# Who makes the low parts of two raw weight blocks, in a fast block product of a decoder layer

## The chip, the cores and the metric

The kernel runs on one core of a Trainium2 chip. The metric is the time of one execution in microseconds (us). TensorE (PE in the profile, PEld its weight loads) multiplies, VectorE (DVE) and ScalarE (ACT) work on SBUF and PSUM, GpSimd (POOL) on SBUF, and SyncE (SP) issues nearly all transfers.

## The reference, cut to what matters

One decoder layer over 1024 rows of width 1024. The part that matters here is a set of dense products, and what is done to their results:

```python
u = rmsnorm(x, norm_mix) @ w_in          # retention gate rg, LRU lx and ly, branch gates: columns of w_in
hl = rg_lru_branch(lx, ...); o_l = hl * gelu(ly)
merged = (g[:, :, 0] * (od @ w_branch[0]) + g[:, :, 1] * (o_r @ w_branch[1])
          + g[:, :, 2] * (o_l @ w_branch[2]))
x = x + merged @ w_out
```

Everything is float32. Attention, retention, cross-attention and the squared-ReLU MLP stand before and after these products and are not touched.

## The kernel before, in words

**Three passes.** A float32 product is made of reduced-precision matmuls: each operand is split into a high part, which is a cast on ScalarE (line 70), and a low part, the operand minus its high part, which is one subtraction (line 71) on an engine that the caller names. Each 128-row step is then three matmuls in a row (lines 59 to 61): high by high, high by low of the right operand, low by high of the left one. So the third matmul of a product is the first that needs the low part of the weights.

**Seven products for eight.** From about 660 us to 1510 us of the span the products are made in pairs of weight units. A pair is a 2x2 arrangement of raw blocks A11, A12, A21, A22 of 128x512 elements; instead of eight block products there are seven (numbered k = 1 to 7), with sums of blocks as left operands. Product 1 uses A11 itself, product 2 uses A12, product 4 uses A22, and products 5, 6, 7, 3 use the sums S1, S2, S3, S4. Each product is four steps of three matmuls into one PSUM tile; six such tiles go round.

**The sums.** `left` (line 1064) makes the four sums on VectorE: S1 = A21 + A22 into a tile of its own; S3 = A11 - A21 over A21; S2 = S1 - A11 over A11; S4 = A12 - S2 over A12. Two of the raw blocks, A11 and A12, are thus overwritten by S2 and S4. S2 can only be written when the high and the low part of A11 have been made, S4 when those of A12 have been.

**Low parts.** `pair` (line 1082) passes the engine `lo` on to `product` (line 1104) and that to `pair_unit` (line 1094), which splits the left operand. In the input projections `lo` is GpSimd for all seven; in the branches (`branch`, line 792) it is VectorE for products 6 and 4 and GpSimd for the other five.

**The results.** `product` combines the seven PSUM tiles on VectorE as they come (lines 1125, 1127 and 1130 add PSUM to an SBUF tile of sums, ScalarE copies the first at line 1121) and hands the four blocks of the output to `emit`. A PSUM tile is free again when VectorE has read it.

**Order of the pairs.** There are 23 pairs in the projections: four for the retention gate, eight for the LRU (every second one from the third on) and eleven for the branch gates; then 12 pairs in the three branches, four each. In the steady part the seven products run in the order 1, 2, 6, 7, 5, 4, 3; where two pairs share each right-hand block (the first and the last two pairs of the projections, and two pairs of each branch) in the order 1, 2, 3, 7, 6, 5, 4. Between LRU pairs stands the recurrence: ScalarE makes sigmoids (line 633), GpSimd a product (line 634), ScalarE tanh, exp and sqrt with table loads (lines 635 to 637), VectorE lines 638 and 639, the scan (line 640) and line 641.

**Order on the queues.** The kernel is written in a framework whose planner sets the order of the instructions on each engine from its own estimates when the kernel is built; from then on each engine takes its queue in that order, and waits where an input is not ready. The casts of the weight units are tied to each other in the order of the source. Raw blocks come through three staging tiles; SyncE's queue holds the load of the next unit until a staging tile has been read for the last time.

Of the kernel before, what the change touches and what calls it, by code (L numbers as in the profile page):

```python
# [49 lines left out]
class Kernel:  # L50
# [1031 lines left out]
    def pair(self, p, k, c, units, right, psum, emit, lo):  # L1082

        if k == 1:
            st = self.sf[:, 6:8, :].rearrange("p k c -> p (k c)") if p % 2 else None
            c["w"] = self.raw_pair(units, st)
            c["t"] = self.sf[:, 2 * p % 4, :], self.sf[:, 2 * p % 4 + 1, :]
        if "left" not in c and 1 in c and 2 in c:
            c["left"] = True
            w = c["w"]  # L1090
            self.left(w, self.sf[:, 4 + p % 2, :], w["A11"], w["A12"], self.nc.vector)
        self.product(k, c, right, psum, lo, emit)

    def pair_unit(self, src, lo):
        if self.n_units % 2 == 0:
# [302 lines left out]
```

## Time and profile before

| | us |
|---|---|
| median of three runs | 2461.78 (2456.99 to 2462.23) |
| the profiled execution | 2457.39 |
| its span, first to last instruction | 2455.6 |
| TensorE busy in it | 2320.9 (95%) |
| VectorE busy | 1854.2 (76%) |
| GpSimd busy | 1091.8 (44%) |
| ScalarE busy | 1044.8 (43%) |

Busy time is what an engine spends in instructions; a wait for another engine is not counted. The granted clock (PEclk) is the share of TensorE's full clock that it was given. Names as `wu<-st` are the tile written and the tiles read: `wu` is a split weight unit, `st` a staging tile, `sf` the tile that holds sums, every second pair's second unit and the partial results.

### The profile page before, as it was taken

The numbers are of one execution on the slowest core, as the hardware profiler recorded it, in microseconds if no ns is written. First come the engines' busy times: TensorE is split into PE (matmuls) and PEld (weight loads), VectorE is DVE, ScalarE is ACT, GpSimd is POOL, SyncE is SP. The second block draws the span as 40 slices with busy tenths as digits, with TensorE's granted clock in tenths as the row PEclk, the third lists the DMA queues.
The fourth block names the chain that finished last, engine by engine and source line by source line (L and its number), as shares of the span: only waits on it lengthen the run. The fifth ranks groups of instructions, "written<-read, shape, count | busy, mean of one in ns | idle before, by whom it ended". The sixth has DMA issues, their size and how long they took to land. (4 is left out here: it accounts for less than half of the span.)

```text
span 2455.6 us, 31231 instructions
## 1 busy us (share of the span) xinstructions
PE 2320.9 (95%) x11132; PEld 1908.8 (78%) x11132; DVE 1854.2 (76%) x2850; ACT 1044.8 (43%) x1823; POOL 1091.8 (44%) x714
## 2 busy tenths in 40 slices
PE   9999999999998999999998987999989999999996
PEld 7888878888876877777876766788768888778884
DVE  7677387877786776786677898345788888788888
ACT  5444355555545454445244443135432222343333
POOL 1122212221216555566542334034155555698787
PEclk9999999999999999999999988999999999999999
DMA  4222222222225345453676776343325444734431
GB/s 170 80 86 70 65 61 69 66 64 62 61 56 195 119 162 171 140 178 112 208 252 211 256 263 193 112 162 104 106 80 175 150 156 141 274 138 172 158 138 74
DMA packets 137259, 338.28 MB, mean 138 GB/s; under 512 B 17152, under 2 KB 27393, under 8 KB 137104
## 3 DMA queue, kind: packets, MB, share of 16 engines
q1 hardware_dynamic: 136528, 334.44, 41.4%
q8 instruction: 89, 1.46, 0.2%
q10 hardware_dynamic: 576, 1.84, 0.2%
q14 instruction: 66, 0.54, 0.1%
HBM read 229.21 MB, written 98.63 MB: 134 GB/s over the span
## 5 line engine op out<-in xcount | busy, mean ns | idle before, releaser
L59 PE MATMUL ps<-block,wu 128*128 128x512 f32 x1428 | 570.7, 400 | 53.8 <-DVE sf L1125 21.5
L61 PE MATMUL ps<-block,wu 128*128 128x512 f32 x1428 | 567.8, 398 | 11.4 <-POOL wu L71 6.2
L60 PE MATMUL ps<-block,wu 128*128 128x512 f32 x1428 | 564.4, 395 | 1.7 <-POOL block L71 1.0
L71 POOL TENSOR_TENSOR wu<-st,wu 128x512 fp32r<-128x512 f32 x214 | 323.3, 1525 | 317.5 <-ACT wu L70 317.4
L59 PEld LDWEIGHTS ps<-block,wu 128*128 128x128 f32 x1428 | 272.9, 191 | 118.1 <-issue 19.5
L61 PEld LDWEIGHTS ps<-block,wu 128*128 128x128 f32 x1428 | 272.8, 191 | 79.2 <-POOL wu L71 11.0
L60 PEld LDWEIGHTS ps<-block,wu 128*128 128x128 f32 x1428 | 272.9, 191 | 62.8 <-DVE block L71 1.6
L70 ACT CAST wu<-st 128x512 fp32r<-128x512 f32 x240 | 141.2, 618 | 166.6 <-DVE st L1066 71.3
L71 POOL TENSOR_TENSOR w<-st,w 128x1024 fp32r<-128x1024 f32 x50 | 123.7, 2485 | 158.3 <-ACT w L70 158.2
L59 PE MATMUL ps<-wu,hu 128*128 128x512 f32 x448 | 177.2, 395 | 17.1 <-DVE acc L1198 14.3
L61 PE MATMUL ps<-wu,hu 128*128 128x512 f32 x448 | 174.8, 392 | 3.6 <-DVE hu L71 3.6
L60 PE MATMUL ps<-wu,hu 128*128 128x512 f32 x448 | 175.5, 392 | 0.0
L1198 DVE TENSOR_TENSOR acc<-acc,ps 128x512 f32<-128x512 f32 x216 | 137.8, 678 | 20.4 <-PE ps L61 19.9
L71 POOL TENSOR_TENSOR wu<-sf,wu 128x512 fp32r<-128x512 f32 x63 | 116.7, 1866 | 67.9 <-ACT wu L70 57.3
L71 DVE TENSOR_TENSOR hu<-sth,hu 128x1024 fp32r<-128x1024 f32 x56 | 121.1, 2167 | 20.9 <-ACT hu L70 20.2
L466 ACT ACTIVATE p<-sc,mx 128x256 f32<-128x256 f32 (+7 forms) x128 | 94.8, 741 | 71.1 <-DVE mx L463 49.2
L59 PEld LDWEIGHTS ps<-wu,hu 128*128 128x128 f32 x448 | 84.7, 189 | 41.3 <-DVE acc L1198 12.4
L61 PEld LDWEIGHTS ps<-wu,hu 128*128 128x128 f32 x448 | 84.7, 189 | 22.6 <-DVE hu L71 4.9
L59 PE MATMUL psk<-block,w 128*128 128x512 f32 x256 | 101.7, 397 | 0.0
L61 PE MATMUL psk<-block,w 128*128 128x512 f32 x256 | 101.2, 395 | 0.0
L60 PE MATMUL psk<-block,w 128*128 128x512 f32 x256 | 100.8, 394 | 0.0
L60 PEld LDWEIGHTS ps<-wu,hu 128*128 128x128 f32 x448 | 84.7, 189 | 17.2 <-POOL wu L71 0.4
(389 smaller groups left out, 5608.0 us busy)
## 6 DMA issues: line engine op xcount, KB each, us to landing
sth<-h SPq DMA_DIRECT2D x56, 512.0 KB, 9.4
st<-in_w SPq DMA_DIRECT2D x32, 512.0 KB, 4.3
h<-hab SPq DMA_DIRECT2D x32, 512.0 KB, 2.8
w<-in_w SPq DMA_DIRECT2D x8, 2048.0 KB
sgb<-gsp SPq DMA_DIRECT2D x48, 256.0 KB, 4.4
gsp<-l SPq DMA_DIRECT2D x44, 256.0 KB, 2.1
acc<-y SPq DMA_DIRECT2D x40, 256.0 KB, 3.8
st<-in_w_br SPq DMA_DIRECT2D x18, 512.0 KB, 5.5
```

The source lines that it names most:

```text
L59: nc.tensor.matmul(ps, lhsT=lhs.hi, rhs=rhs.hi, start=start, stop=False)
L60: nc.tensor.matmul(ps, lhsT=lhs.hi, rhs=rhs.lo, start=False, stop=False)
L61: nc.tensor.matmul(ps, lhsT=lhs.lo, rhs=rhs.hi, start=False, stop=stop)
L70: ins = self.nc.scalar.copy(dst.hi, src)
L71: self.lo_ins = (lo_engine or self.nc.vector).tensor_tensor(dst.lo, src, f32(dst.hi), op=ALU.subtract)
L466: nc.scalar.activation(p[:, 0:n], sc[:, 0:n], AF.Exp, bias=mx, accum_out=l)
L1198: eng.tensor_tensor(acc[k][:, st, :], acc[k][:, st, :], x if isinstance(x, bass.AP) else acc[x][:, st, :], op=ALU.add)
```

## The change: what it does

In `pair`, the engine that makes the low part becomes VectorE where k is 1 or 2, whatever the caller passed; for the other five products it stays what it was. 35 pairs with two products each are concerned, so 70 subtractions of 128x512 elements. The MLP does not go through `pair` and keeps its engines.

```diff
         if "left" not in c and 1 in c and 2 in c:
             c["left"] = True
             w = c["w"]
             self.left(w, self.sf[:, 4 + p % 2, :], w["A11"], w["A12"], self.nc.vector)
-        self.product(k, c, right, psum, lo, emit)
+
+        self.product(k, c, right, psum, self.nc.vector if k in (1, 2) else lo, emit)
```

## Rows read from the trace of the kernel before

**Rows 1.** The page, part 1: busy us, share of the span, instructions.
```profile
PE 2320.9 (95%) x11132; PEld 1908.8 (78%) x11132; DVE 1854.2 (76%) x2850; ACT 1044.8 (43%) x1823; POOL 1091.8 (44%) x714
```

**Rows 2.** Stretches: from:to, length, busy per engine, PEclk, DMA share, GB/s.
```profile
880.00:1170.00 290.00, 269.06 (x1113) 214.32 (x1112) 217.45 (x230) 142.88 (x201) 174.24 (x108) 0.96 0.44 149
...
1236.00:1530.00 294.00, 259.57 (x1088) 209.12 (x1087) 241.15 (x286) 131.16 (x198) 107.88 (x66) 0.94 0.71 236
```

**Rows 3.** TensorE's waits, 880 to 1170 us: us in all, times, longest.
```profile
PE ps L59 <- DVE sf L1130: 15.2, 6, 2.6
```

**Rows 4.** TensorE's waits, 1170 to 1530 us.
```profile
PE ps L59 <- DVE sf L1125: 21.5, 4, 10.3
```

**Rows 5.** VectorE's waits, 660 to 1512 us.
```profile
DVE st L1066 <- POOL wu L71: 78.4, 28, 8.0
```

**Rows 6.** VectorE in order of time, about 934 to 945 us: start, us, what, idle before.
```profile
934.40 1.21 DVE L1066 TENSOR_TENSOR st<-sf,st 128x512 f32<-128x512 f32 x1 [7.99 <-POOL wu L71]
...
936.67 0.69 DVE L1066 TENSOR_TENSOR sf<-st 128x512 f32<-128x512 f32 x1 [0.45 <-DMA st<-in_w_lru]
...
940.34 1.21 DVE L639 TENSOR_TENSOR xc<-xc,g 128x1024 f32<-128x1024 f32 x1
942.71 1.76 DVE L1066 TENSOR_TENSOR st<-st 128x512 f32<-128x512 f32 x1 [1.16 <-POOL wu L71]
944.39 3.38 DVE L640 TENSOR_TENSOR_SCAN g<-r,xc 128x1024 f32<-128x1024 f32 x1
```

**Rows 7.** GpSimd in the same stretch.
```profile
929.45 2.41 POOL L634 TENSOR_TENSOR xc<-g,xc 128x1024 f32<-128x1024 f32 x1 [5.39 <-ACT g L633]
931.81 2.56 POOL L71 TENSOR_TENSOR wu<-st,wu 128x512 fp32r<-128x512 f32 x2
```

**Rows 8.** ScalarE in the same stretch.
```profile
929.26 1.14 ACT L70 CAST wu<-st 128x512 fp32r<-128x512 f32 x2
...
940.03 1.13 ACT L70 CAST wu<-st 128x512 fp32r<-128x512 f32 x2
```

**Rows 9.** SyncE's issues in the same stretch.
```profile
926.86 6.61 SPq L1077 DMA_DIRECT2D st<-in_w_lru  x2
```

**Rows 10.** TensorE in order of time: its starts after a wait.
```profile
942.73 0.50 PE L61 MATMUL ps<-block,wu 128*128 128x512 f32 x1 [1.14 <-POOL wu L71]
950.67 0.50 PE L59 MATMUL ps<-block,wu 128*128 128x512 f32 x1 [2.61 <-DVE sf L1130]
...
1240.71 0.47 PE L59 MATMUL ps<-block,wu 128*128 128x512 f32 x1 [1.54 <-DVE sf L1125]
```

**Rows 11.** Stretches of TensorE alone: from:to, length, busy, PEclk, DMA share, GB/s.
```profile
950.97:954.39 3.42, 3.42 (x10) 0.50 0.88 281
...
1238.00:1245.00 7.00, 4.90 (x21) 1.00 0.86 306
```

**Rows 12.** Groups, 660 to 1512 us: times | busy us, mean ns | idle before.
```profile
L71 POOL TENSOR_TENSOR wu<-st,wu 128x512 fp32r<-128x512 f32 x158 | 238.2, 1525 | 249.7 <-ACT wu L70 249.6
...
L71 DVE TENSOR_TENSOR wu<-st,wu 128x512 fp32r<-128x512 f32 x18 | 20.2, 1120 | 9.3 <-ACT wu L70 9.3
```

**Rows 13.** Low parts that VectorE makes already, whole span: ns least/median/most.
```profile
L71 DVE TENSOR_TENSOR wu<-st,wu x26: 674/685/1786, 1253.9 to 1818.2; 128x512 fp32r<-128x512 f32 x26
```

**Rows 14.** VectorE in order of time, 1234 to 1244 us.
```profile
1234.62 3.46 DVE L71 TENSOR_TENSOR block<-sto,block 128x1024 fp32r<-128x1024 f32 x2
1239.27 0.69 DVE L1066 TENSOR_TENSOR st<-sf,st 128x512 f32<-128x512 f32 x1 [1.19 <-POOL wu L71]
...
1242.30 1.22 DVE L71 TENSOR_TENSOR block<-sto,block 128x1024 fp32r<-128x1024 f32 x1 [1.73 <-ACT block L70]
```

**Rows 15.** VectorE, then ScalarE and GpSimd, about 1472 to 1476 us.
```profile
1474.93 1.77 DVE L1066 TENSOR_TENSOR st<-st 128x512 f32<-128x512 f32 x1 [3.88 <-POOL wu L71]
...
1471.64 1.66 ACT L70 CAST wu<-st 128x512 fp32r<-128x512 f32 x3 [0.63 <-DMA st<-in_w_br]
...
1472.34 3.82 POOL L71 TENSOR_TENSOR wu<-st,wu 128x512 fp32r<-128x512 f32 x3 [9.38 <-ACT wu L70]
```

## The prediction

> **What bounds the kernel now.** I read the page's busy shares first. TensorE is busy 95% of the span and VectorE, the next, 76% [rows 1], so a change that touches neither's amount of matmuls can only win what TensorE stands idle or runs slow. Then I looked at two parts of the stretch in which pairs are made [rows 2]. In the steady part with LRU pairs, 880 to 1170 us, TensorE is busy 269.06 of 290.00 us at a mean clock of 0.96; from the end of the projections through the branches, 1236 to 1530 us, it is busy 259.57 of 294.00 us at 0.94. Next, who ends TensorE's waits. In the LRU part it is VectorE: line 1130, which frees a PSUM tile, ends 15.2 us in six waits of at most 2.6 [rows 3]. In the branches line 1125 ends 21.5 us in four waits, one of 10.3 us [rows 4].
>
> So VectorE's lateness is what TensorE pays for, and VectorE in turn waits for GpSimd: 78.4 us in 28 waits of its sums on a low part [rows 5]. These are exactly the waits that the change aims at: S2 waits for the low part of A11, S4 for that of A12. One wait of each kind stands in the stretch from 934 to 951 us, the pattern of five of the six waits on line 1130. VectorE sits idle 7.99 us before S2 at 934.40; ScalarE had made the two casts concerned by 929.26 + 1.14 = 930.40, but GpSimd was at line 634 until 931.86 and then made two low parts one after the other until 934.37 [rows 6 to 8]. The second of them is that of A11. Then S4 at 942.71 is 1.16 us late behind the low part of A12, and takes 1.76 us instead of the 0.69 us of the sum at 936.67. TensorE waits for the same low part (1.14 us, until 942.73) and then, until 950.67, 2.61 us for line 1130 [rows 6, 10].
>
> A wait costs more than its length. Right behind it the granted clock is 0.50, that is 1.2 GHz instead of 2.4, for 3.4 us in which 1.7 us worth of matmuls gets done [rows 11]; there are six such stretches from 903 to 1159 us. After the wait of 1.54 us at 1240.71 the clock stayed at 1.00 [rows 10, 11].
>
> **The change part by part.** It takes 70 subtractions from GpSimd, at a mean of 1.525 us [rows 12], some 107 us, and gives them to VectorE. There one takes 0.674 to 1.786 us, with a median of 0.685 [rows 13]. So VectorE gets at least 70 x 0.674 = 47 us and at most 70 x 1.786 = 125 us. The 18 that it makes up to 1512 us already have a mean of 1.12 us [rows 12], beside GpSimd at work, which would be 78 us; since 70 of GpSimd's instructions go, I take the median, 70 x 0.685 = 48 us, and add a delay by GpSimd only where one is in sight. Against it stand the 78.4 us of waits, of which only the part behind ScalarE's cast is left. No instruction is added, no transfer and no copy; the casts stay on ScalarE, and the new wait is VectorE's for the cast, which the sum behind it had to outlast anyway.
>
> What VectorE gains is not what TensorE gains, so I go place by place.
>
> First wait of the LRU pattern (S2 at 934.40). The cast ends at 930.40, VectorE makes the low part until 931.09, and S2 starts 3.3 us earlier. But little comes of it: the next sum, S1 of the following pair at 936.67, waits for its raw block [rows 6]. SyncE issued that load only at about 933, in the row of two issues that lasts from 926.86 to 933.47, when GpSimd's other low part (of product 3, which stays there) had freed the staging tile [rows 7, 9]. GpSimd still has line 634 in front of it. The 3.3 us turn into a wait for a transfer. I book nothing.
>
> Second wait (S4 at 942.71). The cast of A12 ends at about 940.63, half of the 1.13 us of the two casts from 940.03 [rows 8]; VectorE is in line 639 until 941.55. Low part and S4 then come one after the other. If both run free, the scan starts at 941.55 + 0.685 + 0.69 = 942.93 instead of 944.39: 1.5 us earlier. If both run into GpSimd's low parts of the next products, as S4 did, it is 941.55 + 1.786 + 1.76 = 945.10: 0.7 us later. I take the low part free and S4 half held, at (0.69 + 1.76) / 2 = 1.23: 941.55 + 0.685 + 1.23 = 943.47, and the scan, line 1130 and TensorE's restart at 950.67 all come 0.92 us earlier. TensorE's own wait for the low part moves inside this and is not counted again. Five such places: 5 x 0.92 = 4.6 us (between 5 x 1.5 = 7.5 won and 5 x 0.7 = 3.5 lost). The sixth wait on line 1130 follows other sums: nothing. I leave the clock's slow stretches where they are: TensorE gets to the wait of 2.61 us some 0.4 us sooner, so it shrinks to 2.61 - 0.92 + 0.4 = 2.1, and the sixth wait, of 15.2 - 5 x 2.6 = 2.2 us, has such a stretch behind it too.
>
> Start of the branches. S2 at 1239.27 waits 1.19 us for GpSimd, and line 1125 behind it releases TensorE at 1240.71 [rows 10, 14]. VectorE's two block subtractions end at 1238.08; without a GpSimd low part beside the second (3.46 us for the two, where the one at 1242.30 took 1.22) about 0.7 us sooner. Then the low part, 0.685, and S2: at 1238.1 instead of 1239.27. Won: 1.1 us.
>
> Late in the branches. S4 at 1474.93 waits 3.88 us for three low parts in a row on GpSimd, of which the second is its own; ScalarE's casts were done at 1473.30 [rows 15]. On VectorE two of the three would be done by 1473.6, S4 by 1474.3 instead of 1476.70, less 0.7 us for the third: 1.7 us won.
>
> The rest of the branches. 24 of the 70 subtractions lie there; VectorE is busy 241.15 of 294.00 us [rows 2], so they don't all find a gap. 24 x 0.685 = 16.4 us are added. The same VectorE instructions cost 1.76 us beside GpSimd's low part and 0.69 us without [rows 6], and 24 GpSimd instructions go: if half of them held one up by 1 us, 12 us come back. Of the difference, 4.4 us, part lies in VectorE's waits for transfers; I put a third, 1.5 us, on the path. Bounds: 24 x 1.12 = 27 us late, or nothing late and the 12 us won.
>
> Sum: 4.6 + 1.1 + 1.7 - 1.5 = 5.9 us won. The profiled execution took 2457.39 us (span 2455.6 and 1.8 around it), so 2451.5 for the like of it; the median of three runs is 4.4 us above it, which makes 2455.9, said as 2456.
>
> A rule that speaks against the change: VectorE's instruction with two SBUF inputs is long where GpSimd works beside it, 1.76 us for S4 against 0.69 us [rows 6]. The Trainium skill (Perfetto Trace Analysis, Optimizing Scalar/DVE Operations) says that the two engines share an SBUF read port, so moving work between them might not help. By that rule the gain would be nil, the third case below; the trace agrees that they hold each other up, but the moved instruction is also shorter there, 0.685 us for 1.525 [rows 12, 13], and that is why I do not follow it.
>
> **The rivals.** (1) The slow stretches of the clock go too: if the waits on line 1130 fall under 1.6 us in five places, 5 x 1.7 = 8.5 us come on top, 14.4 us in all: 2447 us. For it: 1.54 us without a slow stretch; against it: I see only 0.5 us less per place. (2) Nothing comes of it: what VectorE saves it waits for transfers and casts, as S1 at 936.67 shows; within 3 us of before, 2461. (3) Slower, by the queue: the planner sets a new order, and if it puts the low part of A12 ahead of what now stands between 936.67 and 942 us on VectorE (S1, S3, the PSUM readers of lines 1125 and 1127, lines 638 and 639), all of this waits for the cast that ends at 940.63. Low part and S4 would be done at 942.0, the 4.9 us from 936.67 to 941.55 come after that, and the scan starts at 946.9: 2.5 us later per place, 5 x 2.5 = 12.5 us, 2474; it decides from the point where more than 944.39 - 942.0 = 2.4 of the 4.9 us stand behind that wait. In the branches the same order (a low part ahead of PSUM readers, behind a cast that waits for its transfer) would cost up to the 27 us. Against it: line 638's own input comes from ScalarE ahead of that cast.
>
> **How the numbers follow.** Forecast 0.45, rival 1 0.15, rival 2 0.18, rival 3 0.22. What a measurement of this kernel can tell from no change is about 0.2%, 4.9 us. Two thirds of the forecast's chance lie beyond it: faster 0.45 x 0.67 + 0.15 = 0.45; within: 0.45 x 0.33 + 0.18 = 0.33; slower 0.22. The forecast alone spans 2449 to 2460. The range reaches to rival 1 and most of rival 3: 2444 to 2471.
>
> **What would show it.** Right: 88 low parts `wu<-st` on VectorE instead of 18 up to 1512 us, none of its sums waiting on GpSimd for more than 1 us, VectorE's idle time before S2 ended by a cast or gone, line 1130's waits shorter by some 0.5 us. Wrong: those waits as long as before (rival 2), clock at 1.00 behind them (rival 1), or VectorE's low parts with long waits for casts in front of PSUM readers (rival 3). The prediction falls if 1236 to 1530 us changes by more than 10 us either way.

## The result

The changed kernel takes 2446.88 us (median of five runs, 2446.03 to 2450.84) against 2462.23 us of the kernel before on the same chip (2456.99 to 2462.57): a ratio of 0.9946, 95% interval 0.9931 to 0.996, estimated from all runs (the two medians alone would give 0.9938). Run once more on another chip, nothing altered, it had 0.9959 [0.9947, 0.9972]. So it is faster by 0.4 to 0.5%, some 10 to 13 us; the forecast was 6.

The profiled execution of after took 2450.84 us, the slowest of its five. Traces of before (2457.39) and after therefore differ by 6.6 us only, half of what the medians show; the rest has to come from timed experiments. The page, part 1, after:

```profile
PE 2312.1 (94%) x11132; PEld 1901.4 (78%) x11132; DVE 1885.1 (77%) x2920; ACT 1043.4 (43%) x1823; POOL 997.8 (41%) x644
```

70 instructions have gone from GpSimd to VectorE, which is 31 us busier; GpSimd is 94 us less busy [rows 1]. The groups of the low parts from 0 to 1512 us, after (times | busy us, mean ns | idle before):

```profile
L71 POOL TENSOR_TENSOR wu<-st,wu 128x512 fp32r<-128x512 f32 x88 | 139.5, 1595 | 318.5 <-ACT wu L70 275.0 <-DMA st<-oTs 14.2 <-DMA sgb<-gsp 11.7
...
L71 DVE TENSOR_TENSOR wu<-st,wu 128x512 fp32r<-128x512 f32 x88 | 84.8, 978 | 35.1 <-ACT wu L70 35.1
```

All 70 arrived. The mean of VectorE's 88 is 978 ns, for 1525 on GpSimd [rows 12]. VectorE's waits from 660 to 1512 us:

```profile
DVE wu L71 <- ACT wu L70: 35.1, 13, 4.4
...
DVE sf L1066 <- DMA st<-in_w_lru: 19.7, 8, 3.3
DVE sf L1066 <- DMA st<-in_w_gate: 12.6, 3, 5.7
...
DVE sf L1066 <- POOL wu L71: 1.9, 2, 1.2
```

The wait that the change aims at, that of S2 and S4 (`st L1066`), 78.4 us in 28 times [rows 5], is gone altogether. The 1.9 us left are another wait, of sums written to `sf`, which had 3.4 us in two times before. New are the 35.1 us that VectorE's low parts wait for their casts, 9.3 before [rows 12]. Now the stretches in which TensorE could gain from it, after (columns as in [rows 2]; the first is the tail of the attention with the first pairs):

```profile
689.00:751.00 62.00, 60.72 (x325) 48.02 (x324) 53.11 (x102) 32.27 (x69) 12.63 (x12) 1.00 0.21 56
880.00:1170.00 290.00, 264.67 (x1131) 210.64 (x1130) 235.75 (x257) 145.03 (x204) 142.93 (x84) 1.00 0.45 150
1236.00:1530.00 294.00, 258.44 (x1083) 207.88 (x1081) 250.58 (x312) 133.38 (x200) 76.39 (x45) 0.95 0.72 240
```

and the first of them before:

```profile
689.00:751.00 62.00, 56.95 (x304) 44.81 (x304) 49.74 (x92) 30.62 (x65) 13.83 (x13) 1.00 0.19 56
```

From 689 to 751 us TensorE does 3.8 us more work. In the LRU pairs the clock went from 0.96 to 1.00 and TensorE was busy for 4.4 us less [rows 2]: what the clock gave back became idle time. TensorE's waits there, from 880 to 1170 us after, and then those from 1170 to 1530 us:

```profile
PE ps L61 <- DVE wu L71: 9.9, 5, 2.5
PE ps L59 <- DVE sf L1131: 5.9, 6, 1.8
PE ps L61 <- POOL wu L71: 5.4, 5, 1.1
PE ps L59 <- ACT wu L70: 4.2, 4, 1.2
```

```profile
PE ps L59 <- DVE sf L1126: 16.1, 2, 8.1
...
PE ps L59 <- ACT wu L70: 3.6, 1, 3.6
PE ps L59 <- ACT block L70: 3.0, 1, 3.0
...
PE ps L61 <- DVE wu L71: 2.4, 1, 2.4
```

Line 1131 (line 1130 of before, moved down by one) ends 5.9 us instead of 15.2 [rows 3], as hoped, but 9.9 us behind VectorE's own low parts and 4.2 us behind casts are new. In the branches line 1126 (before 1125) ends 16.1 us instead of 21.5 [rows 4]; in a second profile of the same kernel (under experiments, the changed kernel once more) it ends 22.1.

**Why the LRU pairs gained nothing.** One period of two pairs holds 180 matmuls. It is measured from the first `psr` matmul of one LRU gate to that of the next (TensorE alone: from:to, length, busy, clock, DMA share, GB/s). Before, a long and a short period:

```profile
916.22:963.89 47.67, 43.65 (x181) 0.96 0.49 167
1058.74:1100.71 41.97, 41.76 (x181) 1.00 0.45 149
```

After, the same two:

```profile
918.12:965.79 47.67, 42.34 (x181) 1.00 0.51 168
1060.83:1102.08 41.25, 41.25 (x181) 1.00 0.48 159
```

and the first of them in the second profile of the same changed kernel:

```profile
916.19:963.69 47.50, 43.92 (x182) 0.96 0.50 168
```

47.67, 47.67 and 47.50 us, whoever makes the low parts and whatever the clock: 4.0, 5.3 or 3.6 us of idle time fill up what the matmuls leave. So something else sets the period, and 41.25 us is what it is when nothing does. ScalarE shows what. Its waits at line 633, where the LRU gate writes `r` and `g`, from 820 to 1170 us, before and after:

```profile
ACT L633 <- DMA oTs<-r: 15.3, 3, 5.1
ACT L633 <- DVE l L675: 5.1, 1, 5.1
```

```profile
ACT L633 <- DVE g L748: 12.1, 2, 6.0
...
ACT L633 <- DMA oTs<-r: 7.3, 1, 7.3
ACT L633 <- DVE sf L1066: 6.4, 1, 6.4
```

Four waits of 5 us before and of 6 to 7 us after (in the second profile 4.8 to 6.5). The names after the arrows differ, because the profile puts a wait down to what ended last before it; lines 675 and 1066 write neither `r` nor `g`. What the waits have in common is the store: in both profiles all four end 2.8 to 3.6 us after SyncE issued the last store of `r`, as long as such a store takes to land (a median of 2.8 us). Where line 633 did not wait, that store, if there was one, had been issued 10.5 us or more before. The tiles `r` and `g` have one buffer each and two users: the gate (lines 627 to 641) and `o_sums` (line 742), which loads two rows of blocks into them, subtracts, and stores them to `oTs`. A call can load them only when the gate's lines 640 (`r`, until 901.17 here) and 641 (`g`) have let go of them, and the next gate's line 633 only when the last store of `r` has landed. SyncE's issues for the two calls between the gates at 880 and 928 us, after:

```profile
901.25 0.33 SPq L745 DMA_DIRECT2D r<-orT  x1
...
909.15 0.37 SPq L750 DMA_DIRECT2D oTs<-r  x1
...
911.94 0.32 SPq L745 DMA_DIRECT2D r<-orT  x1
...
923.77 0.37 SPq L750 DMA_DIRECT2D oTs<-r  x1
```

Two calls take from 901.25 to some 927 us, while the gate's own matmuls were done by 921.1. VectorE's load is not the reason: it is busy 38.11 of the 47.67 us of this period, and 37.45 of the 41.25 us of the short one. What VectorE does in the meantime, after (compare [rows 6]):

```profile
932.30 1.98 DVE L71 TENSOR_TENSOR wu<-st,wu 128x512 fp32r<-128x512 f32 x1 [4.44 <-ACT wu L70]
934.39 1.61 DVE L1066 TENSOR_TENSOR st<-sf,st 128x512 f32<-128x512 f32 x1
...
939.21 0.69 DVE L1066 TENSOR_TENSOR sf<-st 128x512 f32<-128x512 f32 x1 [2.62 <-DMA st<-in_w_lru]
...
942.94 1.22 DVE L639 TENSOR_TENSOR xc<-xc,g 128x1024 f32<-128x1024 f32 x1
944.07 1.76 DVE L71 TENSOR_TENSOR wu<-st,wu 128x512 fp32r<-128x512 f32 x1
945.75 3.37 DVE L640 TENSOR_TENSOR_SCAN g<-r,xc 128x1024 f32<-128x1024 f32 x1
...
952.42 0.68 DVE L1066 TENSOR_TENSOR st<-st 128x512 f32<-128x512 f32 x1
```

S2 starts at 934.39, before at 934.40, though this gate began 1.9 us later (918.12 for 916.22). The low part of A12 stands exactly where S4 stood, takes the 1.76 us that S4 took, and S4 went behind the scan.

### The profile page after: what moved, and what is told of

Read it like the earlier page. It is cut to its first block, busy times and chain, and to the rows that moved or that the text cites. A ratio compares the mean times of both kernels' runs of the same rounds, so it can differ in the third digit from the quotient of the medians.

```text
span 2448.9 us, 31204 instructions
## 1 busy us (share of the span) xinstructions
PE 2312.1 (94%) x11132; PEld 1901.4 (78%) x11132; DVE 1885.1 (77%) x2920; ACT 1043.4 (43%) x1823; POOL 997.8 (41%) x644
## 4 chain that ended last, share of the span: by engine, by line
PE 51%; DVE 20%; DMA 11%; issue 8%; POOL 5%; ACT 4%; SPq 0%; DVEq 0%; POOLq 0%; ACTq 0%
PE ps L61 7%; PE ps L59 7%; PE ps L60 7%; POOL wu L71 3%; PE psq L59 2%; PE psq L61 2%; PE psq L60 2%; PE sc L458 2%; PE psk L61 2%; DVE block L71 2%; PE psk L60 2%; PE psk L59 2%; DVE acc L1199 2%; DMA st<-oTs 1%; PE psv L60 1%
## 5 line engine op out<-in xcount | busy, mean ns | idle before, releaser
L59 PE MATMUL ps<-block,wu 128*128 128x512 f32 x1428 | 567.6, 398 | 48.3 <-DVE sf L1126 16.1
L61 PE MATMUL ps<-block,wu 128*128 128x512 f32 x1428 | 564.8, 396 | 22.3 <-DVE wu L71 15.2
L71 POOL TENSOR_TENSOR wu<-st,wu 128x512 fp32r<-128x512 f32 x144 | 226.0, 1577 | 385.4 <-ACT wu L70 341.8
L71 DVE TENSOR_TENSOR wu<-st,wu 128x512 fp32r<-128x512 f32 x96 | 90.1, 954 | 35.1 <-ACT wu L70 35.1
L59 PEld LDWEIGHTS ps<-wu,hu 128*128 128x128 f32 x448 | 84.6, 189 | 40.8 <-DVE acc L1199 12.2
L61 PEld LDWEIGHTS ps<-wu,hu 128*128 128x128 f32 x448 | 84.7, 189 | 22.9 <-DVE hu L71 5.1
```

The lines of the kernel that those rows point to most:

```text
L59: nc.tensor.matmul(ps, lhsT=lhs.hi, rhs=rhs.hi, start=start, stop=False)
L61: nc.tensor.matmul(ps, lhsT=lhs.lo, rhs=rhs.hi, start=False, stop=stop)
L71: self.lo_ins = (lo_engine or self.nc.vector).tensor_tensor(dst.lo, src, f32(dst.hi), op=ALU.subtract)
```

## The experiments

Ratios are to the kernel before on the same chip; us worked out from a ratio are taken of 2460.

**One half of the change at a time, by place.** The first kernel:

```diff
@@ branch(): run @@
-                      v if k in (6, 4) else nc.gpsimd)
+                      v if k in (6, 4) else nc.gpsimd, ())
@@ pair(..., lo, raw=(1, 2)) @@
-        self.product(k, c, right, psum, self.nc.vector if k in (1, 2) else lo, emit)
+        self.product(k, c, right, psum, self.nc.vector if k in raw else lo, emit)
```

> The low parts of A11 and A12 on VectorE in the pairs of the projections alone (660 to 1240 us); the branches keep them on GpSimd. The changed kernel took 15 us less than before at the medians. Theory A (the profiles: the stretch with LRU pairs gives nothing, the branches and what follows give it): 2 to 6 us less than before, 2456 to 2460, and each odd LRU pair still has a period of 47 to 48 us. Theory B (the prediction's shares, of 5.9 us 4.6 in the LRU pairs): 10 to 12 us less, 2450 to 2452. Both: the granted clock is 1.00 from 880 to 1170 us.

0.9982 [0.9973, 0.9991], 2452.56 us: 4.4 us less, theory A's range. Its long periods are 47.5 to 49.0 us. The clock expectation that both theories shared was wrong: three half-clock stretches lie between 893 and 962 us, and the periods do not care.

The second kernel has the argument `()` at the call in `h_products` instead.

> The other half: the low parts of A11 and A12 on VectorE in the branches alone (1240 to 1512 us). Theory A: 8 to 12 us less than before, 2450 to 2454, and the six half-clock stretches from 903 to 1159 us are there as before. Theory B: 3 to 5 us less, 2457 to 2459. If neither half gives its share by itself and both do together, the two are not additive and the projections' part pays only with the branches' part.

0.9968 [0.9954, 0.9983], 2451.35 us: 7.9 us less (4.2 to 11.3), nearer to A. The two halves add up to 0.50%, within the change's own 0.41 to 0.54%. A missed a detail: half-clock stretches in the LRU pairs were three in place of six.

**One half at a time, by product.** `k in (1, 2)` becomes `k == 1`, then `k == 2`:

> Only the low part of A11 (product 1, in front of S2) on VectorE, in all pairs. Theory A (the LRU pairs' period is set by the tiles r and g, the gain lies at the start, in the branches and behind them): about half of the change's gain, 4 to 9 us less than before. Theory B (the prediction's booking: the first wait gives nothing but 1.1 us at the start of the branches): 0 to 3 us less.

0.997 [0.9959, 0.9982], 2450.82 us: 7.4 us less.

> Only the low part of A12 (product 2, in front of S4) on VectorE. Theory A: 4 to 9 us less than before, and the two halves add up to the change's 13 us. Theory B (the second wait carries 4.6 + 1.7 of the prediction's gain): 9 to 13 us less. In both the period of the LRU pairs stays at 47 to 48 us.

0.9964 [0.9951, 0.9976], 2449.53 us: 8.9 us less, at the edge between A's range and B's. The first wait is worth as much as the second within the intervals; the prediction's booking of 1.1 us for it in all falls. The two add up to 0.66%, more than the whole change's 0.41 to 0.54%, but not clear of the intervals. The four long LRU periods have 46.6 to 47.9 us in both.

**The cycle over `r` and `g`.** In the changed kernel, then in the kernel before:

```diff
-        sums = {4: [(0, 0)], 6: [(1, 0), (1, 1)], 8: [(1, 2), (1, 3)], 10: [(0, 1), (0, 2)], 12: [(0, 3)],
-                14: [(2, 0), (2, 1)], 18: [(2, 2)], 20: [(2, 3)]}
+        sums = {4: [(0, 0)], 6: [(1, 0)], 8: [(1, 1)], 10: [(1, 2)], 12: [(1, 3)], 14: [(0, 1)], 16: [(0, 2)],
+                18: [(2, 0), (2, 1)], 19: [(0, 3)], 20: [(2, 2), (2, 3)]}
```

> The changed kernel with at most one call of o_sums beside an LRU pair (the second calls of pairs 6, 8, 10 and 14 go to pairs 16 to 20). Theory A (the tiles r and g, which o_sums and the gate share, set the period: ScalarE waits 5 to 7 us at line 633 for the store of r): these waits fall under 1.5 us, the periods of 47 to 48 us fall to 42 to 45, and the time falls 8 to 18 us below the changed kernel, to 2429 to 2439. Theory B (the period is VectorE's own order of work behind the gate, the scan included): the waits at line 633 go, TensorE's waits behind the scan stay, 2444 to 2449.

> The same spread of the calls of o_sums in the kernel before, with all seven low parts on GpSimd. Theory A: as much or nearly as much is won without the change, 8 to 18 us less than before, 2444 to 2454, which would make the cycle the bound in both kernels. Theory C (with r and g free, GpSimd's low parts bind at once): 0 to 4 us less than before, and the change is worth 10 us or more in the LRU pairs once the calls are spread.

0.9907 [0.989, 0.9923], 2434.81 us, which is 0.39 to 0.52% (9.6 to 12.8 us) under the changed kernel, and 0.9962 [0.9949, 0.9975], 2449.93 us. All waits at line 633 are gone in both. A period in the middle, with the change and without:

```profile
996.38:1037.60 41.22, 41.22 (x181) 1.00 0.41 139
```

```profile
1000.18:1042.20 42.02, 41.51 (x181) 1.00 0.42 144
```

Theory A holds: the two calls in one period set it, in both kernels. A second buffer for `r` and `g`, with the calls left where they are, would test the tiles by themselves; no run has it. (The period from 866 to 913 us stays at 47.2 us; there line 633 did not wait, and what sets it was not tried.) Theory B falls, and so does theory C: GpSimd's low parts do not bind at once. In the LRU stretch, from the first gate to the last, 24 us are won with the change (321.0 to 296.9) and 21 without (319.9 to 299.0), and TensorE is never idle in the last four periods of the first. Much is given back where the right side of the first branch is loaded through the same tiles; TensorE's waits from 1195 to 1240 us, with the change and without:

```profile
PE ps L59 <- DVE sf L1126: 10.6, 1, 10.6
```

```profile
PE ps L59 <- DVE sf L1125: 13.9, 1, 13.9
PE ps L59 <- DVE l L675: 1.6, 1, 1.6
PE ps L59 <- DVE sf L1130: 0.7, 1, 0.7
```

So the calls go earlier; in the changed kernel and in the kernel before:

```diff
+        sums = {2: [(0, 0), (0, 1)], 4: [(0, 2)], 6: [(1, 0)], 8: [(1, 1)], 10: [(1, 2)], 12: [(1, 3)],
+                14: [(0, 3)], 16: [(2, 0)], 18: [(2, 1)], 19: [(2, 2)], 20: [(2, 3)]}
```

> The changed kernel with the calls of o_sums spread in another way: two in pair 2, before the first gate, one in each of the pairs 4 to 18 with even numbers, one in 19 and 20. Three calls in place of five (with the calls spread before) lie between 1115 and 1210 us, where TensorE had one wait of 10.6 us behind line 1126. Theory A (that wait is the moved calls' price): it falls under 6 us, and the time to 2424 to 2431. Rival: the wait is that of the right side's blocks, which are loaded through the same two tiles and now come due 27 us earlier; then it stays, 2432 to 2438.

> The kernel before with the calls of o_sums as in the best version so far (two in pair 2, one in each even pair from 4 to 18, one in 19 and 20), all seven low parts on GpSimd. Theory A: with the cycle over r and g gone the change is worth 0.5 to 1 us in each LRU pair's period (42.0 against 41.3) on top of what it is worth elsewhere, so this kernel takes 13 to 19 us more than the version with the change: 2442 to 2449. Rival: the new places of the calls make GpSimd's lateness harmless too, under 8 us between the two.

0.9892 [0.9877, 0.9907], 2429.53 us with the change: A, though the wait is 6.2 us and not under 6. Without it 0.9921 [0.9908, 0.9935], 2438.79 us: below A's range. The two differ by 0.29%, 7.1 us (some 2 to 12 by the intervals), so the rival is the nearer one; with the calls spread as at first they differ by 0.55%, 13.5 us. The last five periods differ as A said, 41.25 us with the change and 41.8 to 42.3 without.

**The low part of S4 as well.** `k in (1, 2)` becomes `k in (1, 2, 3)`, in the changed kernel and in the one with the early calls. Product 3 has S4 as its left operand; the expectations call it A22, which is that of product 4.

> The changed kernel with the low part of A22 (product 3) on VectorE as well, some 35 more. The prediction said that S1 of the following pair waits for a load that GpSimd's low part of product 3 holds back. If so, this wait (eight of the kind took 19.7 us, three for the gate's weights 12.6 us) falls by half or more. Theory A: the time stays within 4 us of the changed kernel, since the LRU period is set elsewhere and VectorE gets fuller in the branches. Rival (each low part taken off GpSimd brings its share): 5 to 8 us less than the changed kernel.

0.9942 [0.9929, 0.9954], 2443.15 us: 1 to 4 us under the changed kernel, which is theory A's range. VectorE's wait for the LRU weights (660 to 1512 us) is not halved, nor is that for the gate's:

```profile
DVE sf L1066 <- DMA st<-in_w_lru: 17.2, 8, 5.4
DVE sf L1066 <- DMA st<-in_w_gate: 9.5, 3, 4.5
```

Yet the load is held back by the low part of product 3, as the prediction read it, whichever engine makes it. In the changed kernel GpSimd makes it until 935.45 and SyncE issues the load at 935.47; with the third low part on VectorE it is made until 924.92 and the load is issued at 924.95:

```profile
933.69 1.76 POOL L71 TENSOR_TENSOR wu<-st,wu 128x512 fp32r<-128x512 f32 x1
935.47 0.33 SPq L1077 DMA_DIRECT2D st<-in_w_lru  x1
```

```profile
922.42 2.50 DVE L71 TENSOR_TENSOR wu<-st,wu 128x512 fp32r<-128x512 f32 x1 [3.48 <-ACT wu L70]
924.95 0.33 SPq L1077 DMA_DIRECT2D st<-in_w_lru  x1
928.45 0.69 DVE L1066 TENSOR_TENSOR sf<-st 128x512 f32<-128x512 f32 x1 [1.60 <-DMA st<-in_w_lru]
```

On VectorE this low part waits 3.48 us for its cast, which comes behind the gate's line 633 on ScalarE, and takes 2.50 us beside GpSimd's line 634. So the move shortens the wait of the sum S1 from 2.62 to 1.60 us only.

That the time is nearly the same hides two opposite parts in the trace: the LRU stretch is 311.3 us, for 321.0 and 320.6 in the two profiles of the changed kernel, its four long periods 45.9 to 47.0; from the last gate to the last matmul of the branches it is 373.9 us, for 369.9 and 373.1.

> The version with the calls spread early and the low part of A22 (product 3) on VectorE as well. Theory A: the LRU pairs are at 41.25 us with TensorE never idle, so nothing is left to win there; 2424 to 2432, the same within 4 us. Rival: the third low part wins in the branches what it won at the start of the run in the changed kernel (4 us): 2421 to 2425.

0.9857 [0.9843, 0.9871], 2423.88 us: the rival's range, and the fastest version, 35 us below the kernel before. Where the cycle is gone, the third low part brings 0.35%, 8.6 us, for 0.04 to 0.17% with the cycle in place; the intervals are too wide to say that the two differ. The rival is right on the time and not on the place: in the traces the LRU stretch is 5.4 us shorter than without the third low part (295.5 for 300.9, all of it in its first two periods), and from the last gate to the branches' last matmul it is 3.6 us longer (373.4 for 369.8).

**The changed kernel once more.** No edit.

> The changed kernel once more, nothing altered. Its first profile, at 2450.84 us, was 4 us above its median and held a wait of 1.27 us at 640.21 us with a half-clock stretch behind it. Theory A: that place is chance; the second profile is without it, the first matmul of the pairs (1.5 us later than before in the first profile) comes 1 to 3 us earlier than before, and the time is 11 to 15 us less than before. Rival: the place belongs to the new order and is there again.

0.9959 [0.9947, 0.9972], 2448.45 us. The place at 640 us is gone, and the first matmul of the pairs comes 1.2 us earlier than before: A, with a gain a little under its range (10.1 us). Again the profiled run, 2452.23 us, is the slowest of the five.

**The first two pairs alone.**

```diff
+            self.pair(p, k, c, units, H, psum or self.p6(sps), emit, nc.gpsimd, (1, 2) if p < 2 else ())
```

> Only four of the 70 low parts on VectorE: those of A11 and A12 of the first two pairs, which run between 665 and 775 us beside the tail of the attention. In every profile of a kernel with the change in the projections, TensorE is busy some 61 of the 62 us from 689 to 751 us, before 57, and the last sum of squares of the attention ends 4 to 5 us earlier. Theory A (this is the new order of the first pairs' sums among the attention's own work, and all that the projections gain): the last sum of squares ends 3 to 6 us earlier than before, the LRU pairs have 47 to 48 us as before, and the time is 2 to 6 us less. Rival (it comes from the later pairs, whose work is put among the first ones'): nothing at 751 us, and no more than 1 us of the time.

0.9995 [0.9984, 1.0006], 2456.08 us: nothing measurable. In its trace (2451.02 us, the second fastest of twelve runs) the last sum of squares of the attention does end 5.6 us earlier, and the end comes 6.3 us earlier. Theory A is right on the place and wrong on the worth: what this one trace shows at 751 us is not in the median. The 4.4 us of the projections need the other pairs too. Between the last gate (1150 us) and 1231 us the three traces with all pairs changed gain another 1.9 to 3.2 us on before, and this one 0.1; that this is where the 4.4 us are, is argued from traces alone. In the two traces of the changed kernel most of it is taken back a few us later: the wait that ended at 1240.71 before, 1.54 us [rows 10], has 2.97 and 5.85 us there.

## Why the prediction was right, and where not

The direction was right and the size about half of what came: 5.9 us forecast, 10 to 13 measured. The terms are another matter.

**The waits go.** Right: 88 low parts on VectorE, nothing left of the 78.4 us. The 70 cost VectorE some 65 us (84.8 less 20.2 [rows 12]) where the prediction took 48, inside its bounds of 47 to 125. Rival 3's sign is there in part, without its price: the low parts wait for casts, 4.44 us at 932.30 with a PSUM reader (line 675) behind, and the kernel is faster all the same.

**First wait of the LRU pattern, booked at nothing.** Right in these pairs (S2 at 934.39 for 934.40), for half of the reason. S1 does wait for its transfer, 2.62 us, and the load does follow the low part of product 3, as the prediction read. But VectorE's low part is late already, by 4.44 us, for a cast, behind ScalarE's 6.44 us at line 633, which the prediction did not see; and taking product 3's low part off GpSimd left 1.60 us of the 2.62. Over the whole kernel the first wait's half won 7.4 us, where 1.1 was booked.

**Second wait, "five such places: 5 x 0.92 = 4.6 us". This step failed.** The four long periods have 47.1 to 48.0 us after and 47.3 to 47.7 before; nothing was won in them, nor in the whole stretch from the first gate to the last (321.0 and 320.6 us for 319.9). Two things were wrong. The step kept VectorE's order and let S4 follow the low part; the planner gave S4's place to the low part and sent S4 behind the scan. And it took VectorE's scan for the end of the chain, while the period was set by `r` and `g`. The evidence stood in the trace of before: 15.3 us of ScalarE's waits on the store of `r`, which the prediction did not read. With that cycle gone the size comes out close: the five periods up to the last gate have 209.9 us without the change and 207.1 with it, 0.57 us a place, for 0.92 (0.73 with the early calls).

**The slow clock left as it was; rival 1.** The clock did rise to 1.00 in the first profile, and gave nothing: 47.67 us with 5.3 us idle, against 47.50 with 3.6 us idle at 0.96. In these periods TensorE is not what the period waits for, and its slow clock costs nothing. Rival 1's rule fails too. In the second profile its condition is met, no wait on line 1131 being longer than 0.8 us, and five half-clock stretches still lie between 895 and 1059 us. The first of them stands behind a wait of 2.10 us for VectorE's low part (until 894.72); the same wait in the first profile, 2.20 us until 897.94, has none behind it.

```profile
PE ps L59 <- DVE sf L1131: 3.8, 5, 0.8
```

**Start of the branches, 1.1 us.** S2 at 1238.41 for 1239.27, TensorE's restart 0.86 us earlier, 1.24 in the second profile: right for the restart. In the first profile of the changed kernel, and TensorE's restart in the second:

```profile
1237.69 0.68 DVE L71 TENSOR_TENSOR wu<-st,wu 128x512 fp32r<-128x512 f32 x1
1238.41 0.69 DVE L1066 TENSOR_TENSOR st<-sf,st 128x512 f32<-128x512 f32 x1
1239.85 0.47 PE L59 MATMUL ps<-block,wu 128*128 128x512 f32 x1 [2.97 <-ACT block L70]
```

```profile
1239.47 0.76 PE L59 MATMUL ps<-block,wu 128*128 128x512 f32 x1 [5.85 <-DVE sf L1126]
```

But TensorE's wait in front of it grew from 1.54 us: it got there 2.3 and 5.6 us earlier, and all but 0.86 and 1.24 us of that went into the wait.

**Late in the branches, 1.7 us.** S4 at 1471.83 without a wait (1473.51 in the second profile), for 1474.93 after 3.88 us: right in kind.

**The rest of the branches, booked at a loss of 1.5.** Wrong in sign. VectorE got 9.4 us busier (250.58 for 241.15) and not 4.4, so some 6 us came back and not 12; still the branches' half alone won 7.9 us, 5 more than the two terms above. That a third of VectorE's extra work lies on the path was a guess, and a wrong one. Which wait pays the 5 us the traces do not tell: the same kernel's two profiles have 16.1 and 22.1 us behind line 1126.

**Not seen at all.** The tail of the attention: TensorE does 3.8 us more from 689 to 751 us, with four moved low parts near. The planner laid out that tail anew, and a sum that had stood 1.68 us for a transfer ahead of an attention split now stands behind it. The time of the kernel with these four alone does not show the gain.

**The rule on the shared port.** The two engines still hold each other up: VectorE's low part beside GpSimd's took 1.76 us at 944.07. The Trainium skill (Perfetto Trace Analysis, Optimizing Scalar/DVE Operations) warns that moving work between the two might not help. The measurement decides against it here: 70 moved instructions left GpSimd 94 us lighter, VectorE 31 us heavier and the kernel 0.4 to 0.5% faster.

That 5.9 lies as near to 10 to 13 as it does is partly luck: 4.6 us were booked in the LRU pairs, which gave nothing, some 6 to 7 too few in the branches, and the projections' half won its 4.4 us in places that no term has.

## What to carry over

Before a wait's length is booked as a gain, look at a whole period of the loop: if it is the same length with and without that wait, as 47.67 us was, another cycle sets it; here it was a pair of single-buffered tiles that two jobs share, and its wait showed on an engine that is 43% busy. An instruction that moves to another engine under a planner changes the order around it, so what stood behind it must be looked for again. Compare a profile with the times of several runs before its few us are explained: a profiled run was the slowest of five twice here.

## What was not expected of the hardware

Two executions of the same program had a granted clock of 1.00 and of 0.97 over 880 to 1170 us, and the same period. On VectorE a 128x512 low part took 0.68 us alone (at 1237.69), and beside GpSimd 1.98 us (at 932.30) and, with the third low part moved, 2.50 us (at 922.42); the longest before was 1.786 us [rows 13].
